# Six gate pairs as seven products each, with the operand sums made in DRAM

## The chip, the cores and the metric

The kernel runs on one core of one Trainium2 chip. The metric is the device time of one execution in microseconds (us). TensorE (PE) multiplies matrices into PSUM banks of 128x512 float32; VectorE (DVE), ScalarE (ACT) and GpSimd (POOL) work on tiles in SBUF; transfers are issued from the queues of SyncE (SP), ACT and POOL. In the profile, PEld is the loading of TensorE's weights.

## The reference

One hybrid decoder layer over 16 meta tokens and 1024 real tokens, D_MODEL = 1024, all in float32:

```
h = rmsnorm(concat(meta, x)) ;  proj = h @ w_in        # 1024 x 5128
u_pool, z_pool, q, k, v, z_attn, f_logit, g_pool, g_attn = split(proj)
y_pool = causal_multiscale_pool(u_pool) * silu(z_pool) # 4 groups, windows 2, 4, 8, 16
y_attn = forgetting_attention(q, k, v, log_sigmoid(f_logit + b)) * silu(z_attn)
merged = sigmoid(g_pool) * (y_pool @ w_up_pool) + sigmoid(g_attn) * (y_attn @ w_up_attn)
out = rmsnorm(residual + merged @ w_out)               # meta tokens dropped
```

The attention has 8 heads of 64, is causal, and adds a running sum of the log forget gates to each score. The two gates `g_pool` and `g_attn` are 1024 columns of `w_in` each; they are needed for the real tokens only.

## The kernel before, in words

Each float32 operand of a large product is split into a high part and a rest (`hi`, `lo`), and each product is made of three terms, hi·hi, hi·lo and lo·hi. The normalised tokens lie in SBUF transposed, as `hh4[j]` and `hl4[j]`: j is the half of the 1024 model dimensions, each tile holds 4 blocks of 128 dimensions by 1040 tokens. A column chunk of `w_in` (128 columns) is loaded by SP into `raw`, split by ACT (`whi`, L140) and POOL (`wlo`, L124, four pieces of 256), and multiplied in `g_proj` (L152) with 8 blocks x 3 terms = 24 matmuls for each 512 tokens: 48 for a chunk. `raw`, `whi` and `wlo` have two buffers each.

The work runs in these stages.

1. **Start** (to about 60 us): loading and normalising the tokens, the first pair of heads.
2. **Attention**: 16 units, one for each head and half of the tokens; a unit goes over 5 (first half) or 9 (second half) blocks of 128 keys. `qk` makes the scores of a block; ACT adds the gate sum (L581), on the diagonal blocks DVE does it with a causal mask (L579); DVE keeps the running maximum `m` (L588). `maxes` turns `m` into a maximum for each query with DVE transposes, a reduction and six small copies that swap partition halves and quarters (L597, L600). `soft` subtracts it (L612), ACT takes the exponential (L613) and the high part (L616), DVE the rest `pl` (L617), POOL adds up the row sums in `acc` (L625); `av` multiplies with V (L633). `finish` adds the two halves of `po` on DVE (L641) and stores them. The scores of unit i+1 are woven into `soft` of unit i (`merged`).
3. **Fill**: the order of TensorE's instructions is written by hand. Between the attention's steps the class `Fill` hands out single matmuls of other projections, as many nanoseconds as `PACE` times a cost figure of the step, less the step's own matmuls. The figures are 1.04·w+70 for a score step and 1.75·w+130 for a soft step of w columns. The free fill is, in this order: 4 chunks `u`, 4 `zp`, 8 `gp`, 8 `ga` (`f_u`, `f_raw`), whose results go by ACT into `st` (two buffers) and by SP to DRAM. `F.drain()` issues what is left when the attention has ended. The other engines' order is made by a planner from the program's order, dependencies and extra edges (`after`: order only; `behind`: a wait).
4. **Behind the attention**: the four `za` chunks (`f_za`), the pooling mixer (`pool_chain` adds shifted copies on DVE, `pool_split`, `pooled` multiplies), the row sums gathered (`fin`), `attn_norm`, `attn_gate`.
5. **Up projections**: 16 steps `up(j, a)` of 24 matmuls; a gate row is loaded from DRAM, its sigmoid is multiplied in; `G[j]` is the merged result. Sums of blocks of `G` and of `W` (`w_out`) are made on POOL and DVE (`t_first`, `t_second`, `s_first` ...).
6. **Output**: `merged @ w_out` is cut into 2x2 blocks and done by seven block products (n = 0 to 6, L995), not eight; `prep(n+1)` splits the next product's operands; then the residual, the norm and the stores.

Of the kernel before, what the change touches and what calls it, by code (L numbers as in the profile page):

```python
# [31 lines left out]
PACE = 2.05  # L32
# [20 lines left out]
def tile_hybrid_block(ctx, tc, x, meta, norm_g, w_in, b_forget, pool_w, pool_scale,  # L53
# [28 lines left out]
    mask = cst.tile([KB, KB], F32, name="mask")  # L82
    nc.vector.memset(mask, 0.0)
    nc.gpsimd.affine_select(out=mask, in_=mask, pattern=[[1, KB]], compare_op=ALU.is_ge, fill=NEG,
                            base=0, channel_multiplier=-1)
# [234 lines left out]
    def f_u(g):  # L320
# [3 lines left out]
        for c0, c1 in PIECES:  # L324
            ps = yield from g_proj(w, c0, c1)
            st = stg.tile([128, 512], F32, name="st")[:, :c1 - c0]
            nc.scalar.activation(st, ps, AF.Copy)
            nc.sync.dma_start(dt[:, c0:c1], st)
# [205 lines left out]
    for p in range(4):  # L534
        spill["y", p] = dr.tile([128, SEQ], F32, name=f"sp_y{p}")

    class Unit:
# [19 lines left out]
        def qk(self, b):  # L557
# [17 lines left out]
            f0 = max(d1, c0)  # L575
            if d1 > c0:
                j = t0 + c0 - b * KB
                mk = tail if own_keys else mask[:, j:j + d1 - c0]
                nc.vector.scalar_tensor_tensor(s[:kb, c0:d1], ps[:kb, c0:d1], nb_, mk, op0=ALU.add, op1=ALU.add)  # L579
            if f0 < 512:  # L580
                nc.scalar.activation(s[:kb, f0:], ps[:kb, f0:], AF.Identity, bias=nb_)  # L581
# [8 lines left out]
        def maxes(self, extra=0.0):  # L590
# [5 lines left out]
            for a, b in ((0, 64), (64, 0)):  # L596
                nc.vector.tensor_copy(x[a:a + 64], r[b:b + 64])  # L597
            nc.vector.tensor_tensor(r2, r, x, op=ALU.max)
            for a, b in ((0, 32), (32, 0), (64, 96), (96, 64)):
                nc.vector.tensor_copy(y[a:a + 32], r2[b:b + 32])  # L600
# [5 lines left out]
        def soft(self, b):  # L606
# [13 lines left out]
            if b == 1:  # L620
                if c0:
                    nc.gpsimd.tensor_copy(acc[:, :c0], S0[:, :c0])
                nc.gpsimd.tensor_tensor(acc[:, c0:], S0[:, c0:], s[:, c0:], op=ALU.add)
            elif b > 1:
                nc.gpsimd.tensor_tensor(acc[:kb, c0:], acc[:kb, c0:], s[:kb, c0:], op=ALU.add)  # L625
# [10 lines left out]
        def finish(self):  # L636
# [3 lines left out]
            nc.scalar.activation(t[hr], po[lr], AF.Copy)  # L640
            nc.vector.tensor_tensor(t[hr], po[hr], t[hr], op=ALU.add)  # L641
            nc.sync.dma_start(spill["y", self.p][hr, self.q0:self.q0 + 512], t[hr])
# [19 lines left out]
    raws = [(n, j) for n, c in (("zp", 4), ("gp", 8), ("ga", 8)) for j in range(c)]  # L662
# [3 lines left out]
    for key in raws:  # L666
        F.add_free(f_raw(key, cols[key[0]] + 128 * key[1]))

# [13 lines left out]
    for i, u in enumerate(units):  # L682
# [13 lines left out]
        u.finish()  # L696
        if nxt is not None and nxt.p != u.p:
# [45 lines left out]
    def f_za(p):  # L743
        w = w_chunk(COL_ZA + 128 * p)
        za[p] = btile("za")
        for c0, c1 in HALVES:
            ps = yield from g_proj(w, NM + c0, NM + c1)
            evacs.append(nc.scalar.activation(za[p][:, c0:c1], ps, AF.Silu))
# [42 lines left out]
    chains, yls = {}, []  # L791
    pool_chain(3)
    pool_chain(2)
    zp, za = [], {}
    for g in (3, 2, 1, 0):
        zp.append(reload(("zp", g)))
    zp.reverse()
    left = [f_za(p) for p in range(4)]

    def half_raw(g):  # L800
        for _ in range(3 * KO + 1):
            next(g)
# [15 lines left out]
    def gate_row(j, a):  # L818
        t = btile("rl")
        nc.sync.dma_start(t, spill[("gp", "ga")[a], j])  # L820
# [21 lines left out]
    for p in range(3):  # L842
        attn_in(p)
    half_raw(left[0])
    pool_split(3)
    run(left[0])
    split2 = pool_split(2)
    silu(zp[3])
    silu(zp[2])
    fin = sm.tile([128, 384], F32, name="fin", tag="fz", bufs=1)  # L850
    lall = fin[:, :256].rearrange("p (u a j) -> p u a j", u=4, a=4)
    rall = fin[:, 256:320]
    rect = fin[:, 320:].rearrange("p (b r) -> p b r", b=2)
    for p in range(4):
        nc.sync.dma_start(lall[32 * p:32 * p + 32],
# [254 lines left out]
```

## Time and profile before

| | |
|---|---|
| median of 3 runs | 744.66 us (744.38 to 744.8) |
| profiled execution: its time, its span | 743.96 us, 742.2 us |
| busy in the span: PE, PEld | 731.2 us (99%), 622.7 us (84%) |
| busy in the span: DVE, ACT, POOL | 533.2 us (72%), 377.0 us (51%), 332.8 us (45%) |
| DMA | 75.35 MB, mean 102 GB/s |
| granted TensorE clock | 0.997 |

How to read it: busy times are from the profiled execution alone, so sums are made against its 743.96 us; it is 0.70 us under the median. Matmuls are pipelined, so the mean duration of one matmul in a row (some 0.39 us) is longer than the distance from one to the next; a row with the total of many gives the distance.

### The profile page before, as it was taken

To read this page: it belongs to the slowest core of one execution; us is meant where nothing else is said; L and a number is where in the kernel's file an instruction comes from. 1 tells how busy PE (TensorE), PEld (TensorE's weight loads), DVE (VectorE), ACT (ScalarE), POOL (GpSimd) and SP (SyncE) were. 2 spreads that over 40 slices of the span, in tenths; PEclk is the share of its full clock that TensorE was granted. 3 is DMA by queue.
4 is the path that set the end of the run, shared out by engine and by line. 5 is a ranking of instruction groups with operands and counts; after the bars stand their busy time and mean duration, and the time that the engine had idled before them with its cause. 6 is when DMAs were issued, how large, how long until landed. Compare 5 with 4: busy or idle time off the path is not lost.

```text
span 742.2 us, 10619 instructions
## 1 busy us (share of the span) xinstructions
PE 731.2 (99%) x3686; PEld 622.7 (84%) x3686; DVE 533.2 (72%) x991; ACT 377.0 (51%) x736; POOL 332.8 (45%) x390
## 2 busy tenths in 40 slices
PE   8999999999999999999999999999999999999996
PEld 5997999988888898889988888888887888888885
DVE  5653577668779877688797687686288554997975
ACT  6662556446557545556563564452545322526445
POOL 4331235456426446345355383183348043606743
PEclk9999999999999999999999999999999999999998
DMA  9301132231312212222323223229375357360006
GB/s 301 88 15 43 29 86 86 62 98 23 95 48 60 80 50 90 78 53 55 94 66 86 80 80 92 72 81 309 95 201 212 142 200 240 116 224 1 1 0 227
DMA packets 76424, 75.35 MB, mean 102 GB/s; under 512 B 9665, under 2 KB 60865, under 8 KB 76370
## 3 DMA queue, kind: packets, MB, share of 16 engines
q1 hardware_dynamic: 74496, 69.95, 30.8%
q10 hardware_dynamic: 1874, 4.72, 1.7%
q8 instruction: 29, 0.48, 0.3%
q14 instruction: 25, 0.20, 0.1%
HBM read 55.58 MB, written 19.07 MB: 101 GB/s over the span
## 4 chain that ended last, share of the span: by engine, by line
PE 87%; DVE 5%; ACT 1%; issue 1%; POOLq 0%; POOL 0%; ACTq 0%
PE pj L152 65%; PE pj L995 8%; PE po L633 5%; PE ps L573 2%; PE ps L572 2%; PE pt L995 2%; PE pj L486 1%; DVE S L612 1%; DVE pl L617 1%; DVE ka L266 0%; PE pj L279 0%; DVE pt L603 0%; ACT S L581 0%; DVE mt L593 0%; ACT whi L140 0%
## 5 line engine op out<-in xcount | busy, mean ns | idle before, releaser
L124 POOL TENSOR_TENSOR wlo<-raw,whi 128x256 fp32r<-128x256 f32 x148 | 121.7, 852 | 192.5 <-ACT whi L140 96.1
L152 PE MATMUL pj<-hh,whi 128*128 128x512 f32 (+4 forms) x768 | 178.4, 360 | 0.6 <-ACT hh L201 0.3
L152 PE MATMUL pj<-hl,whi 128*128 128x512 f32 (+4 forms) x768 | 177.1, 359 | 0.0
L152 PE MATMUL pj<-hh,wlo 128*128 128x512 f32 (+4 forms) x768 | 174.4, 358 | 0.0
L152 PEld LDWEIGHTS pj<-hh,wlo 128*128 128x128 f32 x768 | 132.3, 188 | 18.1
L152 PEld LDWEIGHTS pj<-hh,whi 128*128 128x128 f32 x768 | 131.5, 188 | 18.7 <-ACT hh L201 0.5
L152 PEld LDWEIGHTS pj<-hl,whi 128*128 128x128 f32 x768 | 131.6, 188 | 17.7
L617 DVE TENSOR_TENSOR pl<-S,ph 128x512 fp32r<-128x512 f32 (+4 forms) x112 | 87.1, 792 | 19.3 <-ACT ph L616 18.8
L625 POOL TENSOR_TENSOR acc<-acc,S 128x272 f32<-128x272 f32 (+4 forms) x80 | 76.7, 958 | 11.2 <-ACT S L613 6.0
L581 ACT ACTIVATE S<-ps,negc 128x400 f32<-128x400 f32 (+2 forms) x96 | 49.3, 515 | 44.0 <-DVE S L579 35.7
L613 ACT ACTIVATE S<-S 128x512 f32<-128x512 f32 (+4 forms) x112 | 49.5, 478 | 33.7 <-DVE S L612 33.5
L616 ACT ACTIVATE ph<-S 128x512 fp32r<-128x512 f32 (+4 forms) x112 | 52.2, 480 | 15.8 <-PE po L633 14.4
L588 DVE TENSOR_TENSOR m<-m,S 128x272 f32<-128x272 f32 (+4 forms) x80 | 41.3, 517 | 23.8 <-ACT S L581 22.0
L140 ACT ACTIVATE whi<-raw 128x1024 fp32r<-128x1024 f32 x37 | 39.1, 1056 | 32.2 <-PE pj L152 27.8
L612 DVE TENSOR_TENSOR S<-S,pt 128x512 f32<-128x512 f32 (+4 forms) x112 | 51.9, 498 | 0.8
L836 DVE TENSOR_TENSOR rl<-pj,rl 128x512 f32<-128x512 f32 x32 | 22.0, 689 | 28.0 <-PE pj L152 28.0
L579 DVE SCALAR_TENSOR_TENSOR S<-ps,negc,mask 128x128 f32<-128x128 f32 (+2 forms) x72 | 23.7, 330 | 22.5 <-PE ps L573 22.3
L317 ACT ACTIVATE st<-pj 128x512 f32<-128x512 f32 x40 | 23.7, 593 | 28.1 <-PE pj L152 18.6
L633 PE MATMUL po<-pl,V 128*128 128x512 f32 (+4 forms) x112 | 37.6, 336 | 0.1
L573 PE MATMUL ps<-ql,ka 128*128 128x512 f32 (+4 forms) x112 | 37.5, 334 | 0.0
L572 PE MATMUL ps<-qa,ka 128*128 128x512 f32 (+4 forms) x112 | 36.0, 322 | 0.6 <-ACT S L581 0.5
L995 PE MATMUL pj<-opy 128*128 128x512 f32 (+1 forms) x168 | 36.3, 375 | 0.0
(187 smaller groups left out, 1134.2 us busy)
## 6 DMA issues: line engine op xcount, KB each, us to landing
raw<-in_w_in_dram SPq DMA_DIRECT2D x40, 512.0 KB, 3.9
sp_gp<-st SPq DMA_DIRECT2D x16, 256.0 KB, 2.0
sp_ga<-st SPq DMA_DIRECT2D x16, 256.0 KB, 2.0
rl<-sp_gp SPq DMA_DIRECT2D x8, 512.0 KB, 5.2
rl<-sp_ga SPq DMA_DIRECT2D x8, 512.0 KB, 4.5
W<-in_w_out_dram SPq DMA_DIRECT2D x8, 512.0 KB, 4.8
xr<-in_x_dram SPq DMA_DIRECT2D x8, 512.0 KB, 4.1
xt<-in_x_dram SPq DMA_DIRECT2D x7, 512.0 KB, 8.1
```

The lines of the kernel that those rows point to most:

```text
L124: ins = nc.gpsimd.tensor_tensor(out[:, c:c + 256], x[:, c:c + 256], y[:, c:c + 256], op=op)
L152: nc.tensor.matmul(ps, a, b, start=(i == 0), stop=(i == len(seq) - 1))
L572: nc.tensor.matmul(ps[:kb, c0:], ka[:, k0:k0 + kb], qa[:, q0 + c0:q0 + 512], start=True, stop=False)
L573: nc.tensor.matmul(ps[:kb, c0:], ka[:, k0:k0 + kb], ql[:, q0 + c0:q0 + 512], start=False, stop=True)
L581: nc.scalar.activation(s[:kb, f0:], ps[:kb, f0:], AF.Identity, bias=nb_)
L612: nc.vector.tensor_tensor(s[:kb, c0:], s[:kb, c0:], self.pm[:kb, c0:], op=ALU.subtract)
L613: exps.append(nc.scalar.activation(s[:kb, c0:], s[:kb, c0:], AF.Exp))
L616: nc.scalar.activation(ph[:kb, c0:], s[:kb, c0:], AF.Copy)
L617: dves.append(nc.vector.tensor_tensor(pl[:kb, c0:], s[:kb, c0:], r32(ph[:kb, c0:]), op=ALU.subtract))
L625: nc.gpsimd.tensor_tensor(acc[:kb, c0:], acc[:kb, c0:], s[:kb, c0:], op=ALU.add)
L633: nc.tensor.matmul(self.po[:, c0:], v, r[:kb, c0:], start=(b == 0 and i == 0), stop=(b == self.nb - 1 and i == 1))
L995: nc.tensor.matmul(ps, pick(A_, k, p)[:, i * 128:(i + 1) * 128], pick(B_, k, q)[:, c0:c1], start=start and n == 0, stop=n == 11, skip_grou ...
```

## The change

**Gates.** The 8 pairs of gate chunks (`gp` j, `ga` j) are cut: pairs 0 to 5 (`NP = 6`) are no longer two chunks of 48 matmuls. A pair is a 2x2 block product: rows gp and ga, the model dimension in two halves, the tokens in two halves. It is done by seven products of 12 matmuls (4 blocks x 3 terms, 512 tokens): A11·B11 (`q1`), A12·B21 (kept as `c11`), SD4·B22 (`x`), SD2·TT2, SD1·TT1, SD3·TT3, A22·TT4. Here SD1 = A21+A22, SD2 = SD1+A11, SD3 = A11+A21, SD4 = SD2+A12 are sums of the weights, and TT1 = B11-B12, TT2 = TT1+B22, TT3 = B12-B22, TT4 = TT3-B11+B21 sums of the tokens.

**Sums in DRAM.** `sums_of(i)` runs behind unit i. `put` is a copy from DRAM to DRAM on SP's queue, `add` a transfer on POOL's queue that adds onto its destination. The negated token halves (`negative`) are made by 12 DVE instructions of 128x512 through `st`. The same is done for the sums of `w_out` (TD1 to TD4), which were POOL's work in SBUF before; in the output stage the signs change to match. In all there are 17 `add`s for the sums, 4 that add the two halves of `po` (which `finish` now stores apart), and 6 in `join` behind the attention.

**Where the products go.** In the fill: 4 `u`, 4 `zp`, 4 `za`, 2 `gp`, 2 `ga` chunks, then SD4·B22 for two pairs at a time (`f_q3`, 3 times) and `q1`, `c11` (`f_q12`, 6 times); each of these nine has one weight split for 24 matmuls. Behind the attention: `t_prep` loads TT2, TT1, TT3, TT4 and overwrites the token halves with their splits; then 12 phases of 24 matmuls, with a weight split each, whose results are combined on DVE (`phase`) and stored; the pooling mixer and the norms are given out over the phases by the lists `todo` and `late`. `f_za` is gone from there.

**Off VectorE.** The mask is an `affine_select` on POOL after ACT's copy, except on a unit's own-keys block; the six swaps of `maxes` are ACT copies; the add in `finish` is gone. `PACE` goes from 2.05 to 1.7.

```diff
-PACE = 2.05
+PACE = 1.7
+NP = 6
...
+    def g_prod(w, n, kh, th, ps=None):
+        ...
+        t = slice(NM + 512 * th, NM + 512 * th + 512)
+        for i, (a, b) in enumerate((a, b) for a, b in ((0, hh4), (0, hl4), (1, hh4)) for _ in range(4)):
+            k = i % 4
+            nc.tensor.matmul(ps, w[a][:, 4 * n + k, :], b[kh][:, k, t], start=first and i == 0, stop=i == 11,
+                             skip_group_check=True)
+            yield mm_ns(512)
+        return ps
+    def f_q12(j):
+        w = w_chunk(COL_GP + 128 * j)
+        for n, key in enumerate(("q1", "c11")):
+            ps = yield from g_prod(w, n, n, 0)
+            keep(part[key][:, j], ps)
+    def f_q3(jj):
+        w = split_w([s_cols(4, 2 * jj), s_cols(4, 2 * jj + 1)])
+        for n in range(2):
+            ps = yield from g_prod(w, n, 1, 1)
+            keep(part["x"][:, 2 * jj + n], ps)
+        free_from.append(stores[-1])
...
+    def put(dst, src):
+        after(nc.sync.dma_start(dst, src), stores[-1])
+    def add(dst, src, **kw):
+        after(nc.gpsimd.dma_start(dst, src, accum_op=ALU.add, **kw), accs[-1])
+    def sums_of(i):
+        if i == 0:
+            put(SD[1], GB[2])
+            put(SD[3], GB[0])
+        elif i == 1:
+            add(SD[1], GB[3])
+        elif i == 2:
+            add(SD[3], GB[2])
+            put(SD[2], SD[1])
+            negative(TT[1], 0, 1)
+        ...
+        elif i == 8:
+            add(TT[2], side_h(hh4, 1, 1))
+            add(TT[4], TT[0], max_dma_last_dim=4096)
+        ...
+        if i % 4 == 3:
+            add(spill["y", i // 4], spill["yl", i // 4], max_dma_last_dim=4096)
...
-            if d1 > c0:
-                ...
-                nc.vector.scalar_tensor_tensor(s[:kb, c0:d1], ps[:kb, c0:d1], nb_, mk, op0=ALU.add, op1=ALU.add)
-            if f0 < 512:
-                nc.scalar.activation(s[:kb, f0:], ps[:kb, f0:], AF.Identity, bias=nb_)
+            if own_keys:
+                nc.vector.scalar_tensor_tensor(s[:, c0:], ps[:, c0:], nb_, tail, op0=ALU.add, op1=ALU.add)
+            else:
+                nc.scalar.activation(s[:, c0:], ps[:, c0:], AF.Identity, bias=nb_)
+                if d1 > c0:
+                    nc.gpsimd.affine_select(out=s[:, c0:d1], in_=s[:, c0:d1], pattern=[[1, d1 - c0]], ...)
...
-                nc.vector.tensor_copy(x[a:a + 64], r[b:b + 64])
+                nc.scalar.activation(x[a:a + 64], r[b:b + 64], AF.Copy)
...
+    def t_prep(n, kh, th):
+        t = slice(NM + 512 * th, NM + 512 * th + 512)
+        for h in range(2):
+            s = gp.tile([128, 2, 512], F32, name="ts", tag="g")
+            after(nc.sync.dma_start(s, TT[n][:, 2 * h:2 * h + 2]), free_from[-1])
+            hi = hh4[kh][:, 2 * h:2 * h + 2, t]
+            nc.scalar.activation(hi, s, AF.Copy)
+            nc.vector.tensor_tensor(hl4[kh][:, 2 * h:2 * h + 2, t], s, r32(hi), op=ALU.subtract)
+    PH = ((2, 0, 1), (1, 1, 1), (3, 0, 0), (None, 1, 0))
+    def phase(jj, i):
+        w = phase_weights(jj, i)
+        ...
+            if i == 0:
+                tt_(X[:, n], X[:, n], ps, op=ALU.subtract)
+            elif i == 1:
+                tt_(X[:, n], X[:, n], ps, op=ALU.add)
+            elif i == 2:
+                tt_(U[:, n], a, Q1[:, n], op=ALU.subtract)
+                tt_(U[:, n], U[:, n], R[jj][5 + n], op=ALU.subtract)
+            else:
+                tt_(Q1[:, n], a, Q1[:, n], op=ALU.subtract)
+        if i:
+            nc.sync.dma_start(part[("c12", "c22", "c21")[i - 1]][:, two], (X, U, Q1)[i - 1])
+    def join(jj):
+        two = slice(2 * jj, 2 * jj + 2)
+        for key in ("x", "c11"):
+            after(nc.gpsimd.dma_start(part[key][:, two], part["q1"][:, two], accum_op=ALU.add), los[-1])
...
+    todo = [[("split", 3), ("chain", 2)], [], [("silu", 3), ("gather",)], [("pooled", 3), ("split", 2), ("silu", 2)],
+            [("chain", 1), ("zp", 1)], [("pooled", 2), ("split", 1), ("ain", 0)], [("chain", 0), ("norm", 0), ("zp", 0)],
+            [("pooled", 1), ("split", 0), ("ain", 1), ("norm", 1), ("za", 0)]]
+    late = [[("gate", 0), ("ain", 2), ("norm", 2), ("za", 1)], [("pooled", 0), ("gate", 1), ("ain", 3), ("za", 2)],
+            [("norm", 3), ("gate", 2), ("za", 3)], [("gate", 3)]]
+    for n in range(count):
+        phase(n // 4, n % 4)
+        if n % 2 and 0 < (n + 1) // 2 < NP // 2:
+            join((n + 1) // 2)
+        for t in plan[n]:
+            fn[t[0]](*t[1:])
...
-        W[k] = hq.tile([128, D], F32, name="W", tag="w")
-        after(nc.sync.dma_start(W[k], wout[:, k, :]), muls[-1])
+    WSRC = [WB["11"], WB["21"], TD[2], TD[1], TD[3], WB["22"], TD[4]]
+    def w_load(n, h):
+        W[n, h] = hq.tile([128, 2, 512], F32, name="W", tag="w")
+        return nc.sync.dma_start(W[n, h], WSRC[n].rearrange("(k p) c -> p k c", p=128)[:, 2 * h:2 * h + 2])
```

More of the change, by code (lines that the diff above doesn't have):

```diff
@@ L696, in tile_hybrid_block @@
         u.finish()
+        sums_of(i)
         if nxt is not None and nxt.p != u.p:
@@ L791, in tile_hybrid_block @@
     chains, yls = {}, []
-    pool_chain(3)
[L793 to L802, printed above, removed]
+    def join(jj):
+        two = slice(2 * jj, 2 * jj + 2)
+        for key in ("x", "c11"):
+            after(nc.gpsimd.dma_start(part[key][:, two], part["q1"][:, two], accum_op=ALU.add), los[-1])
+    join(0)
+    t_prep(2, 0, 1)
+    t_prep(1, 1, 1)
+    t_prep(3, 0, 0)
+    t_prep(4, 1, 0)
+    pool_chain(3)
+    zp, za = {}, {}
+    for g in (3, 2):
+        zp[g] = reload(("zp", g))
     def pooled(g):
@@ L840, in up @@
             gt[j] = sg_
[L842 to L855, printed above, removed]
-                          sums[4 * p:4 * p + 4].rearrange("u (a r) j -> r u a j", r=32))
```

243 lines of the change are left out of this document (163 added, 80 removed).

## The prediction

> **What bounds the kernel now.** First the page's busy shares and its chain of waits, then a table of busy time by stage. Its columns: stretch, length, then busy time of PE, weight loads, DVE, ACT, POOL with instruction counts, granted clock, DMA share, GB/s.
>
> ```profile
> span 742.2 us, 10619 instructions
> ...
> PE 731.2 (99%) x3686; PEld 622.7 (84%) x3686; DVE 533.2 (72%) x991; ACT 377.0 (51%) x736; POOL 332.8 (45%) x390
> ...
> PE 87%; DVE 5%; ACT 1%; issue 1%; POOLq 0%; POOL 0%; ACTq 0%
> ```
> ```profile
> 60.00:503.00 443.00, 442.09 (x2274) 384.92 (x2272) 335.19 (x710) 238.21 (x491) 205.70 (x233) 1.00 0.25 70
> 503.00:519.00 16.00, 16.00 (x72) 13.01 (x71) 9.28 (x8) 3.92 (x6) 5.47 (x4) 1.00 0.89 304
> 519.00:569.00 50.00, 50.00 (x218) 40.60 (x217) 31.22 (x28) 22.04 (x29) 27.29 (x25) 1.00 0.50 149
> 569.00:659.00 90.00, 90.00 (x387) 72.03 (x386) 59.78 (x80) 35.43 (x47) 31.95 (x36) 1.00 0.57 197
> 659.00:742.00 83.00, 76.69 (x349) 63.52 (x347) 63.95 (x91) 40.74 (x88) 38.90 (x57) 0.98 0.19 70
> ```
>
> The stages are attention, drain, the work behind it, up projections, output. TensorE is busy for the whole of each but the last few microseconds, at full clock. That a busy TensorE is really what sets the time is read from its waits in the attention, and from a stretch of pure matmuls on the chain:
>
> ```profile
> PE ps L572 <- ACT S L581: 0.5, 1, 0.5
> PE pj L152 <- DVE V L285: 0.2, 1, 0.2
> ```
> ```profile
> 659.04 8.20 PE pj L995 x36
> ```
>
> It waits 0.7 us in 443. One 512-column matmul takes 8.20/36 = 0.2278 us, so the time is a count of matmuls, and taking work off DVE gains nothing by itself: nobody waits for DVE long enough to show. What the change can win is matmuls; what it can lose is this cover.
>
> **The matmuls.** Gates before: 16 chunks x 48 = 768. After: 4 chunks x 48 + 6 pairs x 7 x 12 = 696. That is 72 fewer, 72 x 0.2278 = **-16.4 us**. By place: the fill had 20 chunks (zp, gp, ga) = 960 and gets 12 chunks and 3 x 72 = 792, so -168; behind the attention the za chunks (192) go and 12 x 24 = 288 come, +96 (+21.9 us). Up and output keep their counts. The stages shift: the weave's cost figures sum to 128 us over all steps (37,888 columns of each kind), so 0.35 less PACE takes some 45 us of fill out of it. Counted step by step by the kernel's own rule, 1577 instead of 1782 fill matmuls are handed out before the last unit ends, and 106 instead of 69 are left to drain. So the attention ends 205 x 0.2278 = 46.7 us earlier (503 to 456), the drain takes 24.1 us instead of 15.7, the phases with the four pooling products (312 matmuls) 71.1 us instead of 49.2: up starts at 552, not 568. The stage behind the attention is 95 us instead of 65.
>
> **The attention, engine by engine.** Rows of the groups in 60 to 503 us (count | busy, mean ns | idle before), the select from the start:
>
> ```profile
> L581 ACT ACTIVATE S<-ps,negc 128x512 f32<-128x512 f32 x32 | 21.8, 685 | 8.1 <-PE ps L573 7.8
> ...
> L588 DVE TENSOR_TENSOR m<-m,S 128x512 f32<-128x512 f32 x24 | 18.8, 785 | 11.4 <-ACT S L581 11.0
> L579 DVE SCALAR_TENSOR_TENSOR S<-ps,negc,mask 128x128 f32<-128x128 f32 x48 | 16.7, 347 | 12.2 <-PE ps L573 11.9
> ...
> L600 DVE COPY my<-ms 32x16 f32<-32x16 f32 x64 | 11.2, 175 | 1.1
> ...
> L641 DVE TENSOR_TENSOR t<-po,t 64x512 f32<-64x512 f32 x15 | 10.3, 684 | 0.2
> L581 ACT ACTIVATE S<-ps,negc 128x400 f32<-128x400 f32 x16 | 9.4, 588 | 9.7 <-DVE S L579 9.7
> ...
> L597 DVE COPY mx<-mr 64x16 f32<-64x16 f32 x32 | 8.2, 255 | 0.8
> ...
> L613 ACT ACTIVATE S<-S 128x16 f32<-128x16 f32 x16 | 3.3, 208 | 3.2 <-DVE S L612 3.2
> ```
> ```profile
> L406 POOL TENSOR_TENSOR wlo<-raw,whi 128x1024 fp32r<-128x1024 f32 x3 | 7.1, 2381 | 2.0 <-ACT whi L401 2.0
> ...
> L84 POOL TENSOR_SCALAR_AFFINE_SELECT mask<-mask 128x128 f32<-128x128 f32 x1 | 0.3, 293 | 0.0
> ```
>
> DVE loses 72 masks (48 take 16.7 us; all, at this mean, at most 25), the swaps (19.4) and the 16 adds of `finish` (11), and gains 12 negations (0.785 each, as the nearest two-input row: 9.4). 335 becomes about 290 in 396 us, 73% as against 76%. ACT gains 72 times the 128 columns that DVE took (97 ns for 112 columns by the two rows: 8), 8 blocks more (2), 96 swaps of 0.208 (20): 238 becomes 268, 68% instead of 54%. POOL gains 72 selects x 0.293 = 21.
>
> POOL also issues 21 adding transfers here. No transfer on POOL's queue is in this trace. From below I take SP's issue of one (0.38 us, row further down), from above POOL's longest single operation, 2.4 us (L406): 8 to 50 us; I take 20, since a description of a transfer is nearer to an issue than to 131,072 subtractions. The nine fill chunks of 24 matmuls cost a split of POOL each where 48 used to share one; as four projections' worth less of fill remains, the splits go from 31 to about 28, -10 us. POOL: 206 to some 237, 60%.
>
> So means are no higher than 73%. But the weave is tighter: an odd unit (nine soft steps, five score steps) has cost figures of 8.85 us, so TensorE goes through it in 15.1 us, not 18.1. What it has in hand there is seen in the timeline, for units 13 and 5:
>
> ```profile
> 431.63 0.68 DVE L617 TENSOR_TENSOR pl<-S,ph 128x512 fp32r<-128x512 f32 x1
> ...
> 436.87 0.39 PE L633 MATMUL po<-ph,V 128*128 128x512 f32 x1
> ```
> ```profile
> 230.66 1.69 DVE L617 TENSOR_TENSOR pl<-S,ph 128x512 fp32r<-128x512 f32 x1
> 231.74 0.19 PEld L633 LDWEIGHTS po<-ph,V 128*128 128x128 f32 x1
> ...
> 232.40 0.19 PEld L633 LDWEIGHTS po<-pl,V 128*128 128x128 f32 x1 [0.48 <-DVE pl L617]
> ```
>
> Unit 13 has 4.6 us between `pl` and its use; unit 5, where the next pair's q, k and v also go through DVE, has none. The weave loses 3.1 us, its five masks give back 5 x 0.347 = 1.7: 1.4 us a unit. Unit 13 can pay this, units 5 and 9 can't: 2 x 1.4, taken as **+3 us**. Bounds: 0, and all eight odd units, 11.
>
> **Behind the attention.** Here POOL and DVE get more work in proportion than TensorE: 4.4 chunks of the drain and 12 phases need 16.4 splits in 95 us; before it was four. The question is whether the two can work side by side. Timeline rows, alone and together, and a DVE row alone:
>
> ```profile
> 519.41 2.83 POOL L124 TENSOR_TENSOR wlo<-raw,whi 128x256 fp32r<-128x256 f32 x4 [5.64 <-ACT whi L140]
> ...
> 558.19 6.76 POOL L124 TENSOR_TENSOR yl<-rl,yh 128x256 fp32r<-128x256 f32 x4
> 559.23 5.12 DVE L758 TENSOR_TENSOR y<-y,za 128x1024 f32<-128x1024 f32 x3
> ```
> ```profile
> L777 DVE TENSOR_TENSOR s<-s 128x1025 f32<-128x1025 f32 x1 | 1.2, 1226 | 0.0
> ```
>
> Four POOL pieces alone take 2.83 us, three such DVE operations 3.7: 6.5 together, and side by side they took 6.76. They take turns. The work that takes turns: POOL 16.4 + 4 (the `yl` pieces) times 2.83 = 58, six joins at 0.38, 2; DVE with both inputs in SBUF: 14 in the chains, 4 `pll`, 8 in `t_prep`, 8 norms and gates = 34 x 1.23 = 42. That is 102 us in 95. Some 4 us of norms and gates may slip into the up stage, which wants them only at its fifth step. The phases' 30 combining operations read PSUM and are left out. So 3 to 7, taken as **+5 us**; as low as 0 if turns overlap at their edges.
>
> The Trainium skill, page "SBUF — State Buffer", section "SBUF: two separate sides", has this as a rule: VectorE with two SBUF inputs and GpSimd share a port pair under an exclusive lock, and the loser waits for the whole instruction. By that rule, 102 - 95 = 7 us; these rows agree within 0.3 us in 6.5.
>
> Of transfers, this stage gets (MB): drain loads and stores 4, TT 4.2, u 2.1, zp and za 4.2, y and rc 4.2, phase weights 6.3, X and Q1 3.1, phase stores 4.7, joins 3.1, first up rows 1.6: 37.5. The rate in the busiest stretch before, and SP's rows:
>
> ```profile
> 506.00:522.00 16.00, 16.00 (x71) 12.98 (x70) 6.37 (x5) 5.20 (x6) 8.06 (x8) 1.00 0.94 320
> ```
> ```profile
> raw<-in_w_in_dram SPq DMA_DIRECT2D x40, 512.0 KB, 3.9
> ```
> ```profile
> 499.35 0.38 SPq L136 DMA_DIRECT2D raw<-in_w_in_dram  x1
> ```
>
> 320/0.94 = 340 GB/s when full: 110 us for a stage of 95. About 4 MB can lie outside (two of the four TT, one u before; the last stores behind), which leaves 98 us, hidden beside the turns. A raw chunk takes 3.9 us to land and has two buffers, so it needs no free queue, only one not more than a phase (5.5 us) behind. Bounds 0 and +15. The phases' stores wait on DVE in SP's queue, and the next phases' weights stand behind them: this is where a late DVE reaches TensorE.
>
> **Nothing** is taken for the rest: the W sums leave POOL, which sat at 32 of 90 us in the up stage; loads of W come later in stages with DMA shares of 0.57 and 0.19. They are covered by 387 and 349 matmuls; uncovered, a W load is some 4 us.
>
> **Sum.** 742.2 - 16.4 + 3 + 5 = 733.8 of span; with 1.8 us around it (743.96 less 742.2) 735.6; the median lies 0.7 above the profiled run: **736 us**.
>
> **Rivals.** *Everything is covered*: the matmuls alone, 744.66 - 16.4 = 728. For it: 0.7 us of waits now, means under 75%. Against: unit 5. Chance 0.22. *The transfers bound the stage behind the attention*: 110 us and not 95, +15, +3 in the attention: 746; with each join counted as read and written (3.1 MB more, 9 us) 755. For it: shares of 0.89 and 0.94 already with half the bytes. Against: TensorE did not wait then, and loads can be early. It decides from a stretch of 13 us. Chance 0.17. *POOL's queue holds the attention*, the slower side: the select now stands between ACT's copy and DVE's maximum, and on POOL it can stand behind a split (up to 3.3 us) and an adding transfer (2.4, or longer if its `put` hasn't landed, since the queue is in order). 5.7 us against the 3.2 (4.6 - 1.4) that an odd unit has left: 2.5 x 8 = 20, with the +8 above: 756. Against: splits were in that queue before, and TensorE had 4.6 in hand. It decides from 4.3 us of delay a unit. Chance 0.11. That the change doesn't do what it says is no rival for the matmuls: they are counted out in the code.
>
> **Numbers.** The forecast, with a stretch of 3 to 13 us (731 to 742), has 0.50. About 0.2%, 1.5 us, is what this measurement can tell from no change: same is 743.2 to 746.1. The transfers' case gives 0.02 faster, 0.07 same, 0.08 slower; POOL's 0.01 same, 0.10 slower. Faster 0.74, same 0.08, slower 0.18. The range goes from 727 (all covered, less a little) to 750, which leaves out the far ends of the two slow cases, some 0.15.
>
> **What would show it.** Right: TensorE instructions down by some 72; attention's last `po` near 460; up from about 557 to 562; waits of TensorE on DVE's `pl` in units 5 and 9, on `wlo` or on DVE's combinations in the phases. Wrong: a DMA share near 1 through the phases with loads landing in over 8 us; selects late on POOL and TensorE waiting in `po` in most odd units; or no wait at all.

## The result: 821.26 us, a tenth slower, and the profile after

The kernel after takes 821.26 us (816.69 to 822.97), 1.102 times the kernel before, with a 95% interval of 1.097 to 1.107. The forecast was 736, its range ended at 750. From here on "the stage behind" means the time from the attention's last `po` to the first `up`, that is the drain and the phases.

The page of the kernel after: its first rows, the DMA queues (q0 holds the adding transfers that POOL issues, q1 those of SP's queue), and the chain:

```profile
span 821.3 us, 11051 instructions
PE 741.2 (90%) x3614; PEld 625.1 (76%) x3614; DVE 526.8 (64%) x856; ACT 419.0 (51%) x855; POOL 370.1 (45%) x492
DMA packets 110091, 140.91 MB, mean 172 GB/s; under 512 B 11841, under 2 KB 72257, under 8 KB 109906
q1 hardware_dynamic: 97424, 108.23, 41.9%
q0 software_dynamic: 10160, 25.17, 17.8%
PE 53%; DMA 13%; DVE 8%; POOL 7%; issue 6%; ACT 6%; SPq 1%; POOLq 0%; ACTq 0%; DVEq 0%
```

TensorE has its 72 matmuls fewer (3614, not 3686), yet is busy for 741.2 us. Without any loss its busy time would be 731.2 - 16.4 = 714.8 and its idle time the 11.0 of before (742.2 - 731.2). So the span of 821.3 lies 95.5 above 725.8, in two parts: 69.1 more idle (80.1 against 11.0), and 26.4 of matmuls that took longer. The granted clock answers for the second: it stands at half for 67 us of the span, against 4 before. And transfers are now on the chain with 13%, where there were none.

The table of busy time by stage (us, busy time and count of PE, weight loads, DVE, ACT and POOL, then granted clock, DMA share, GB/s): attention, drain, the hole before the first phase, phases with the pooling.

```profile
60.00:492.00 432.00, 407.65 (x2069) 354.57 (x2068) 303.30 (x537) 257.47 (x587) 230.56 (x314) 0.97 0.63 151
...
492.00:528.00 36.00, 26.68 (x107) 21.01 (x106) 4.91 (x4) 12.69 (x18) 13.68 (x20) 0.91 0.96 294
528.00:539.00 11.00, 0.97 (x5) 0.45 (x3) 2.94 (x3) 2.81 (x4) 0.00 (x0) 0.71 1.03 293
539.00:648.00 109.00, 82.43 (x312) 63.62 (x313) 67.73 (x69) 33.68 (x38) 66.99 (x68) 0.87 0.81 243
```

Each stage against the count of its matmuls: the attention ends at 492 and not at 456; the drain lasts 36 us and not 24.1; then TensorE has nothing for 11 us; the phases last 109 us and not 71.1. That is 36 + 12 + 11 + 38 = 97 us (95.5 by the spans), all of it between the first unit and the first `up`. From the first `up` (648) to the end it is 173 us, as before.

What TensorE waited for, in the same kernel (us in total, times, longest):

```profile
PE pj L915 <- ACT whi L137: 21.2, 4, 10.5
PE pj L336 <- ACT st L343: 9.3, 2, 6.2
PE pj L915 <- DVE U L905: 8.1, 2, 7.4
PE po L743 <- DVE pl L727: 7.7, 8, 1.7
PE ps L681 <- ACT S L687: 6.9, 4, 5.3
```

The two largest are waits of the phases for split weights and of the drain for an evacuation. ACT is not slow there: a split of raw weights takes it 1.05 us, as before. The pieces of transfer in the chain of waits say who is late (start, length):

```profile
158.18 8.58 DMA tt<-st
...
204.06 8.03 DMA tt<-st
...
218.20 6.01 DMA tt<-st
```
```profile
505.75 4.62 DMA part_c<-st
511.10 10.18 DMA part_c<-st
522.01 4.97 DMA part_c<-st
528.09 10.20 DMA raw<-sd
552.23 9.84 DMA u<-sp_u
569.34 10.81 DMA raw<-sd
```

And the list of issues (KB each, median us from issue to landing):

```profile
raw<-in_w_in_dram SPq DMA_DIRECT2D x34, 512.0 KB, 5.2
...
raw<-sd SPq DMA_DIRECT2D x24, 256.0 KB, 4.9
...
tt<-st SPq DMA_DIRECT2D x12, 256.0 KB, 6.0
u<-sp_u SPq DMA_DIRECT2D x4, 520.0 KB, 9.8
```

A chunk of raw weights took 3.9 us before and takes 5.2 now; `u` took 4.9 and takes 9.8. The prediction had named its refutation: a share near 1 through the phases with loads landing in over 8 us. That came in the drain and the hole (0.96, 1.03, raw weights in 10.2 us). In the phases the share was 0.81; there `u` and `Q` (the reloaded `q1`) landed that late (medians 8.1 and 8.9 us), the weights in 5.3, at worst 10.8.

### The profile page after: what moved, and what is told of

Same layout as the page of the kernel before. It is cut to its first block, busy times and chain, and to the rows that moved or that the text cites. A ratio compares the mean times of both kernels' runs of the same rounds, so it can differ in the third digit from the quotient of the medians.

```text
span 821.3 us, 11051 instructions
## 1 busy us (share of the span) xinstructions
PE 741.2 (90%) x3614; PEld 625.1 (76%) x3614; DVE 526.8 (64%) x856; ACT 419.0 (51%) x855; POOL 370.1 (45%) x492
## 3 DMA queue, kind: packets, MB, share of 16 engines
q1 hardware_dynamic: 97424, 108.23, 41.9%
q0 software_dynamic: 10160, 25.17, 17.8%
## 4 chain that ended last, share of the span: by engine, by line
PE 53%; DMA 13%; DVE 8%; POOL 7%; issue 6%; ACT 6%; SPq 1%; POOLq 0%; ACTq 0%; DVEq 0%
PE pj L149 31%; PE pj L1160 7%; POOL wlo L121 4%; PE pj L336 3%; DMA raw<-sd 3%; PE pj L915 3%; PE po L743 3%; DMA tt<-st 3%; DMA part_c<-st 2%; DVE pl L727 2%; PE pt L1160 2%; PE ps L682 1%; DMA tt<-tt 1%; PE ps L681 1%; DMA u<-sp_u 1%
## 5 line engine op out<-in xcount | busy, mean ns | idle before, releaser
L121 POOL TENSOR_TENSOR wlo<-raw,whi 128x256 fp32r<-128x256 f32 x184 | 152.1, 913 | 148.8 <-ACT whi L137 134.8
L149 PE MATMUL pj<-hh,whi 128*128 128x512 f32 (+4 forms) x576 | 130.5, 357 | 4.0 <-DVE S L722 2.4
L149 PE MATMUL pj<-hh,wlo 128*128 128x512 f32 (+4 forms) x576 | 130.5, 353 | 0.0
L149 PE MATMUL pj<-hl,whi 128*128 128x512 f32 (+4 forms) x576 | 128.6, 351 | 0.0
L149 PEld LDWEIGHTS pj<-hh,wlo 128*128 128x128 f32 x576 | 98.8, 193 | 10.0
L149 PEld LDWEIGHTS pj<-hl,whi 128*128 128x128 f32 x576 | 97.5, 191 | 9.9
L687 ACT ACTIVATE S<-ps,negc 128x512 f32<-128x512 f32 (+4 forms) x104 | 57.5, 560 | 33.8 <-PE ps L682 33.1
L915 PE MATMUL pj<-hh,whi 128*128 128x512 f32 x96 | 30.3, 443 | 34.9 <-ACT whi L137 21.2
L915 PEld LDWEIGHTS pj<-hh,whi 128*128 128x128 f32 x96 | 19.6, 212 | 41.9 <-ACT whi L137 28.9
L689 POOL TENSOR_SCALAR_AFFINE_SELECT S<-S 128x128 f32<-128x128 f32 (+2 forms) x72 | 25.7, 391 | 51.1 <-ACT S L687 50.6
L743 PE MATMUL po<-ph,V 128*128 128x512 f32 (+4 forms) x112 | 37.5, 335 | 2.6 <-ACT ph L726 2.6
## 6 DMA issues: line engine op xcount, KB each, us to landing
sd<-in_w_in_dram POOLq DMA_DIRECT2D x4, 1536.0 KB, 13.8
```

The source lines that it names most:

```text
L121: ins = nc.gpsimd.tensor_tensor(out[:, c:c + 256], x[:, c:c + 256], y[:, c:c + 256], op=op)
L149: nc.tensor.matmul(ps, a, b, start=(i == 0), stop=(i == len(seq) - 1))
L687: nc.scalar.activation(s[:, c0:], ps[:, c0:], AF.Identity, bias=nb_)
L743: nc.tensor.matmul(self.po[:, c0:], v, r[:kb, c0:], start=(b == 0 and i == 0), stop=(b == self.nb - 1 and i == 1))
L915: nc.tensor.matmul(ps, w[a][:, 4 * n + i % 4, :], b[kh][:, i % 4, t], start=first and i == 0, stop=i == 11, skip_group_check=True)
```

## The experiments

The table gives the main quantities of all runs. "Transfers" is the busy time of the 16 DMA engines in the stage behind, from the packets' records; for the kernel after it can be worked out from the rows above, share times length: 0.96 x 36 + 1.03 x 11 + 0.81 x 109 = 134 us. The packets' times overlap a little, as the share of 1.03 shows. "Drain" includes the hole before the first phase. The times are medians, the stages come from one profiled execution each. The kernel after ran in 816.7 to 823.0 us and its profile is the slowest of these, so differences of a few us between two rows show nothing by themselves.

| run | time, us | ratio to before | last `po` | drain | phases | transfers |
|---|---|---|---|---|---|---|
| after | 821.3 | 1.102 | 492 | 47 | 109 | 134 |
| b_offv | 747.0 | 1.003 | - | - | - | - |
| a_nosum | 791.2 | 1.062 | 462 | 47 | 107 | 132 |
| a_negput | 799.4 | 1.073 | 470 | 47 | 107 | 132 |
| a_np4 (8 phases) | 818.1 | 1.099 | 484 | 70 | 89 | 131 |
| a_wonce | 789.2 | 1.061 | 493 | 48 | 77 | 111 |
| a_noload | 791.9 | 1.064 | 489 | 47 | 78 | 110 |
| a_notprep | 818.4 | 1.100 | 490 | 34 | 119 | 119 |
| a_lean | 794.9 | 1.068 | 493 | 35 | 92 | 94 |
| a_st4 | 810.3 | 1.090 | 480 | 47 | 108 | 132 |
| a_ahead | 818.1 | 1.099 | 494 | 47 | 105 | 137 |
| a_st4ahead | 808.9 | 1.087 | 482 | 48 | 104 | 139 |
| a_best | 798.5 | 1.072 | 482 | 45 | 98 | 129 |
| a_st4notprep | 804.5 | 1.081 | 482 | 31 | 114 | 119 |
| a_bare | 762.5 | 1.024 | 481 | 29 | 81 | 77 |
| a_barenosum | 742.9 | 0.998 | 463 | 31 | 74 | 73 |

**The masks and swaps alone (b_offv).** The kernel before with the masks and the swaps of "Off VectorE" alone. `PACE` stays 2.05, and `finish` keeps its add:

```diff
-                nc.vector.scalar_tensor_tensor(s[:kb, c0:d1], ps[:kb, c0:d1], nb_, mk, op0=ALU.add, op1=ALU.add)
...
+                nc.scalar.activation(s[:, c0:], ps[:, c0:], AF.Identity, bias=nb_)
+                if d1 > c0:
+                    nc.gpsimd.affine_select(out=s[:, c0:d1], in_=s[:, c0:d1], pattern=[[1, d1 - c0]],
...
-                nc.vector.tensor_copy(x[a:a + 64], r[b:b + 64])
+                nc.scalar.activation(x[a:a + 64], r[b:b + 64], AF.Copy)
```

> The kernel before with only the masks (a select on GpSimd behind ScalarE's copy) and the six swaps (ScalarE) taken off VectorE; PACE 2.05, gates and all transfers as before. Theory T, late transfers (the stores from the two `st` buffers and the weight loads land late because the sums in DRAM and the loads behind the attention crowd the DMA queues; ScalarE and VectorE then wait in order, TensorE idles and runs at half clock after it): no change, 743 to 747 us. Theory P, GpSimd's queue (the select behind splits and sums makes the maximum late): slower by 5 us or more here already, TensorE waiting in po or ps.

746.96 us, 1.0031 [1.0019, 1.0044]: 2.3 us slower, and no wait of TensorE above 1.3 us. A select behind the splits in POOL's queue holds nobody for long. The rival in which POOL's queue holds the attention falls as far as masks and splits go; the adding transfers in that queue are in the next runs.

**The sums in the attention (a_nosum, a_negput).** First without any of them, then with all but the negations:

```diff
 def sums_of(i):
-        if i == 0:                         # a_nosum: every copy, add and negation goes
-            put(SD[1], GB[2])
...
-            negative(TT[1], 0, 1)          # a_negput: a plain copy for each negated half
+            put(TT[1], w_in2[:, :4, 0:512])
...
```

> The changed kernel without any sum in DRAM: no put, no add, no negation; the products read blocks of w_in and w_out in place of the sums (so the numbers computed are others), with the same count of matmuls, splits and of loads behind the attention. Only the four adds of the attention's halves and the joins stay. Theory T: the attention's last po moves from 492 us to 460 to 470, the stage behind it stays near 150 us long (its own loads and stores are all there): about 795 us. Theory P: the selects and the tighter weave remain, so the last po stays above 480: about 810 us.

> The changed kernel with its 12 negations by VectorE left out: the three negated halves are filled by one copy each from DRAM to DRAM (of other data, so the numbers are others), all further sums as they were. Theory T in the form that the shared `st` buffers are the door: the idle stretches of TensorE between 158 and 222 us go, and the attention ends some 15 us earlier: about 805 us. If the traffic as such slows everything, or GpSimd's queue: within 5 us of 821.

Without sums the attention ends at 462, where the prediction had it at 456 + 3. Masks on POOL, swaps on ACT, the tighter weave: those terms of the sum were right within 3 us, in size; where the waits fall is taken up below. The row of its attention, and what TensorE waited for there:

```profile
60.00:462.00 402.00, 397.65 (x2072) 347.61 (x2071) 283.87 (x525) 257.29 (x587) 213.15 (x298) 1.00 0.27 75
```
```profile
PE pj L149 <- DVE S L676: 2.4, 1, 2.4
PE ps L635 <- ACT S L641: 1.1, 3, 0.5
PE po L697 <- DVE pl L681: 0.8, 2, 0.5
```

TensorE idles 4 us there, against 24 with the sums (432.00 - 407.65 above), and the mean clock is 1.00. So the sums cost 30 us, and DVE's share was not the reason (283.87 of 402 against 303.30 of 432). With plain copies of the same size in place of the twelve negations the attention ends at 470: 22 of the 30 us belong to the negations. The other 8 are all that the sums' copies and adding transfers cost it, POOL's queue included. The negations go through the two `st` buffers, which also carry the evacuations of the fill. The rows of the tile `st` in the kernel after, 140 to 240 us (who waited for it, us and times):

```profile
DMA to landing us min/median/max: 1.9/5.2/8.6
```
```profile
  DVE st L593: 11.6, 4
  ACT st L314: 8.7, 1
```

A store from `st` that lands after 5 to 8.6 us keeps a buffer for that long. The next negation on DVE, or the next evacuation on ACT, stands in its engine's queue in front of the soft steps' work, and TensorE waits for those. Both runs came out as theory T has it, a_negput with more than the 15 us expected.

**Four `st` buffers (a_st4).**

```diff
-    gp  = ctx.enter_context(tc.tile_pool(name="gp", bufs=13))
-    stg = ctx.enter_context(tc.tile_pool(name="stg", bufs=2))
+    gp  = ctx.enter_context(tc.tile_pool(name="gp", bufs=12))
+    stg = ctx.enter_context(tc.tile_pool(name="stg", bufs=4))
```

> The kernel after, with four `st` buffers in place of two (negations, y's parts and the products that are kept go through them) and 12 in place of 13 `g` buffers to make the room. Theory B (the two buffers are what the stores' longer landing is felt through): last po at 472 to 480 in place of 492, drain 24 to 30 us in place of 36, the stretch behind as before; 795 to 808. Rival (the DMA engines' bytes set the pace, the buffers only show it): last po 486 to 492 and drain 33 to 37, or what they win comes back in the phases; 814 to 822.

810.28 us, 1.0895 [1.0834, 1.0957]. In the attention, theory B holds: last `po` at 480, 12 us earlier. In the drain it falls: 36 us as before, with a hole of 10 behind. The total lies between the ranges of the two theories. ACT's timeline in that drain shows other releasers, `t_prep`'s loads and a weight load:

```profile
487.14 1.06 ACT L869 ACTIVATE hh<-ts 128x1024 fp32r<-128x1024 f32 x1 [10.44 <-DMA ts<-tt]
...
506.68 1.06 ACT L869 ACTIVATE hh<-ts 128x1024 fp32r<-128x1024 f32 x1 [8.20 <-DMA ts<-tt]
...
525.84 1.06 ACT L137 ACTIVATE whi<-raw 128x1024 fp32r<-128x1024 f32 x1 [9.67 <-DMA raw<-sd]
```

ACT waits in order for a transfer that is not in, and the evacuation that TensorE needs stands behind it. The two stalls cover for each other.

**Without t_prep (a_notprep), and without it and with four buffers (a_st4notprep).** Both leave out `t_prep`, so the phases multiply other numbers.

```diff
-    t_prep(2, 0, 1)
-    t_prep(1, 1, 1)
-    t_prep(3, 0, 0)
-    t_prep(4, 1, 0)
```

> The changed kernel without t_prep: the token sums are not loaded and split behind the attention (the phases multiply the tokens as they are), so 4.2 MB of loads, 8 operations of ScalarE and 8 of VectorE go, nearly all of them from the drain. Theory C: the drain's stores land in 3 us, not 5 to 10, the drain shrinks from 36 to about 26 us and the first phase follows it at once: total 800 to 805. Theory L: the drain shrinks by that, the phases don't: 805 to 812.

> The kernel after with four `st` buffers (12 `g` buffers) and without t_prep, so the phases multiply other numbers than they should. Theory C (each of the two alone left the other to hold the drain): drain 24 to 28 us, last po to up 138 to 148, total 795 to 804. Rival (something third holds the drain): drain 31 us or more, total 804 to 812.

a_notprep: 818.38 us. Drain and hole go from 47 to 34, and the phases from 109 to 119: nearly all is given back, and both theories fall. a_st4notprep: 804.53 us, drain 31.0. Its drain is 3 us shorter than without `t_prep` alone and sits on the rival's edge of 31: the cover was there, but it is not all. A third thing holds the drain; a_barenosum below shows it.

**Weights loaded once (a_wonce), and split each time (a_noload).** In a_wonce the first phase's weights serve all twelve; in a_noload they are loaded once and split anew by ACT and POOL for every phase.

```diff
 def phase_weights(jj, i):
-    n = PH[i][0]
...
-    return split_w([s_cols(n, 2 * jj), s_cols(n, 2 * jj + 1)])
+    if "w" not in R:                                  # a_wonce
+        R["w"] = split_w([s_cols(2, 0), s_cols(2, 1)])
+    return R["w"]
```

> The changed kernel with one weight load and one split for all 12 phases (the later phases reuse the first one's, so the gates computed are others): 11 loads of 0.5 MB, 11 splits of ScalarE and 11 of GpSimd fewer behind the attention, matmuls as before. Now 155 us lie between the last po and the up projections, where 95 us are matmuls. Theory L (a loop of load, ScalarE's split and GpSimd's split over two raw buffers, some 17 us for two phases, sets the pace of the phases): 105 to 115 us, total 770 to 782. Theory C (the bytes crowd all transfers; the loop is only one victim): 130 to 140 us, total 795 to 806.

> The same, but each phase splits anew from one raw tile that is loaded once: the 11 loads are gone, all splits stay. If in the loop the load is the long part (5 to 10 us): close to the kernel with one split, within 8 us. If the turns of GpSimd and VectorE are: it stays 15 us or more above it, near 800 us.

a_wonce: 789.24 us, stage behind 125, between the ranges of both theories. a_noload: 791.90 us, 2.7 above it, as it should be if the load is the long part. The rows of the phases, first a_wonce, then a_noload:

```profile
540.00:617.00 77.00, 75.40 (x312) 60.74 (x313) 56.92 (x67) 22.73 (x28) 23.99 (x24) 0.96 0.84 259
```
```profile
537.00:615.00 78.00, 75.71 (x313) 59.27 (x314) 64.60 (x68) 33.16 (x38) 74.02 (x68) 0.98 0.83 260
```

POOL goes from 24 to 74 us of 78, busy all through, beside DVE with 65, and the phases grow by one and a half us. So the splits and the turns of POOL and DVE, for which the prediction charged 5 us, cost some 1.5 us here. POOL has next to nothing to spare in that stage, so what the turns would cost beside 71 us of bare matmuls is not shown. The eleven loads, 5.8 MB, cost 31 us of phase: the 24 us by which the transfers' busy time falls (134 to 110 in the table), and 7 more.

**Fewer pairs (a_np4), and no joins (a_lean).** a_lean leaves out `t_prep`, the joins, and the loads of X and Q1 (set to zero).

```diff
-NP = 6
+NP = 4                                                # a_np4
```
```diff
-    join(0)                                           # a_lean, beside t_prep; the later joins too
...
-            nc.sync.dma_start(R[jj][0], part["x"][:, two])
+            nc.gpsimd.memset(R[jj][0], 0.0)                 # the same for Q1
```

> The changed kernel with four pairs by seven products, not six (NP = 4): 24 matmuls more than with six (+5.5 us), four phases fewer behind the attention. Theory T: the stage from the attention's end to the up projections shrinks from 155 us in proportion to its loads, by 30 to 40 us, with the attention hardly changed: 785 to 795 us. If the stage behind were bound by VectorE and GpSimd taking turns, as the prediction had it: it shrinks by the turns of four phases, some 12 to 15 us: about 810 us.

> The changed kernel without t_prep, without the six joins and without the loads of X and Q1 (GpSimd zeroes them): 10.4 MB of some 38 fewer behind the attention, three of them in adding transfers; weights and stores stay. Theory C: the stage shrinks from 155 us to 110 to 120: 780 to 787 us. Theory L: weights are the pace still, 135 us or more: 800 us or more.

a_np4, 818.07 us: a third less of the change's products, hardly anything won, and both theories missed. They left out where the matmuls go: the drain has 225 of them, not 105, and the stage 441, not 417. With these and 131 us of transfers it lasts 158, as with six. a_lean, 794.86: the stage falls from 156 to 127, which neither theory had. Its transfers, 94 us, take no longer than its 95 us of matmuls, and it still lost 32 us. So "the longer of transfers and matmuls" is the wrong model.

**Order in SP's queue (a_ahead, a_st4ahead).** In the kernel after, a phase's load can stand behind the store of the phase before. SP's timeline there:

```profile
617.76 0.45 SPq L922 DMA_DIRECT2D rc<-recs  x1
625.32 0.32 SPq L910 DMA_DIRECT2D part_c<-X  x1
...
627.12 1.20 SPq L133 DMA_DIRECT2D raw<-sd  x2
```

By POOL's timeline the raw buffer for phase 10 was free at 612, but the load is issued at 627, behind a store; the store waits for DVE, DVE for the phase before, and phase 10 then starts 7 us after its load is issued (634). a_ahead asks for the weights one phase earlier in the program:

```diff
 def phase(jj, i):
-    w = phase_weights(jj, i)
+    w = pws.pop(0)
+    if 4 * jj + i + 1 < 2 * NP:
+        pws.append(phase_weights((4 * jj + i + 1) // 4, (i + 1) % 4))
```

> The kernel after, with the weights of a phase asked for one phase earlier in the program, ahead of the phase's stores and of the other loads in SP's queue; same transfers, same two raw buffers. Theory O (the order of SP's queue: a load stands behind stores that wait for the phase before): phases 80 to 92 us in place of 108.7; 793 to 806. Rival (bytes: the same transfers take the same time in any order): phases 100 to 112; 813 to 824.

> Both edits of the two runs beside it. Theories B and O together: 768 to 790, last po 472 to 480, drain 24 to 30, phases 80 to 92. Rivals (bytes): above 805.

818.08 and 808.91 us. The phases go from 109 to 105 and 104 us, the totals by less than these kernels scatter: theory O falls, the order of these loads is worth 4 us at most. Waits that vanish at one place turn up at another: in a_ahead those for split weights fall from 21.2 to 13.8 us, those for DVE's `U` rise from 8.1 to 15.2.

**Packets of 1 KB (a_best).**

```diff
-    nc.sync.dma_start(raw[:, k0:k0 + s.shape[1], :], s)      # two of [128, 4, 128]
+    nc.sync.dma_start(raw, src)                              # one of [128, 4, 256]
```

> The run a_st4ahead (808.9 us), and the weights of a pair of chunks loaded as one transfer with runs of 1 KB in place of two with 512 B. 512 B packets took 30.6 ns and 2 KB packets 95.0 ns on queue q1 in the kernel after; 1 KB packets should take 45 to 52 ns in place of 61 for the same bytes, 0.3 to 0.5 us of all engines for each of the twelve loads. Theory S (packets matter): 798 to 806. Rival (no): 806 to 812.

798.53 us, 1.0720 [1.0702, 1.0739], 10 us below a_st4ahead, as theory S has it. 1 KB packets took 54.1 ns in the mean and 46 in the median, against 30.6 and 27 for 512 B: over 7,680 packets and 16 engines that is 3.4 us of engine time in the whole kernel. The gain is larger; half of SP's issues for these loads are gone too, and which of the two brought the rest was not separated. This is the fastest of the variants that do the whole change, and it stays 54 us behind the kernel before.

**Without the transfers (a_bare, a_barenosum).** All matmuls and combinations stay; a_bare is a_lean with four `st` buffers and one weight load and split; a_barenosum also drops the sums, negations included.

> The kernel after with four `st` buffers (12 `g` buffers), without t_prep, without the joins, X and Q1 set to zero in place of their loads, and one weight load and split for all twelve phases: all matmuls and combinations are kept, the numbers are not. About 70 us of transfers are left in the stage, under the 95 us of its matmuls. Theory T (the transfers hold the stage): last po to up 95 to 104 us, last po 478 to 482, total 748 to 760. Rival Q (the queues' order or the engines' turns hold a part of their own): 112 us or more, total 768 or more.

> The run a_bare, and no sums in the attention either (no copies, adding transfers or negations there; the products read blocks of the weights as they are). Theory T: last po 459 to 463, last po to up 95 to 104, total 727 to 738, what the prediction gave with everything covered. Rival: 748 or more.

a_bare: 762.53 us, stage behind 110. That is between the theory's 95 to 104 and the rival's 112. a_barenosum: 742.94 us, 0.9976 [0.9956, 0.9995], stage 104.5; the time lies between the theory's 738 and the rival's 748. A row of its page and its two stages:

```profile
PE 720.3 (97%) x3614; PEld 612.3 (83%) x3614; DVE 490.2 (66%) x836; ACT 400.9 (54%) x836; POOL 312.2 (42%) x431
```
```profile
463.00:495.00 32.00, 28.49 (x115) 22.06 (x114) 7.12 (x8) 11.03 (x17) 22.79 (x27) 0.95 0.78 228
495.00:568.00 73.00, 71.70 (x310) 57.90 (x309) 49.29 (x59) 19.55 (x23) 16.82 (x18) 1.00 0.66 220
```

With these transfers gone the phases are TensorE's again: 71.70 busy of 73, full clock. By the spans, 81 of the 95 us of loss are gone (821.3 to 740.2). Not all of it need be the transfers': the negations, `t_prep`'s work on ACT and DVE and eleven splits went too, and two `st` buffers came. a_noload bounds the splits at some 1.5 us; the rest was not taken apart. What is left, 14.4 us over the matmul count (740.2 against 725.8), is 8.9 of idle time and 5.5 of slower matmuls. The largest single wait is in the drain. ACT's timeline:

```profile
477.15 0.36 ACTq L783 DMA_DIRECT2D rl<-sp_zp  x1
477.61 0.60 ACT L343 ACTIVATE st<-pj 128x512 f32<-128x512 f32 x1 [6.30 <-DMA sp_yl<-t]
```

A reload on ACT's queue takes memory that the attention's last `t` still holds; it waits 6.3 us for the store of `t`, and an evacuation stands behind it, for which TensorE waits 3.2 us. This is the third thing in the drain; in a_st4notprep the same wait took 6.36 us of ACT and 3.3 of TensorE.

## Why the prediction was wrong, by its steps

**The bound** was read rightly for the kernel before: nothing but matmuls. That this cover would carry the change was the error.

**The matmuls**: 72 fewer, as counted. But a kernel with these matmuls, and with most of the change's transfers left out, takes 742.9 us and not 728: the case "everything is covered" was not reached even there: the tighter weave, the drain and the transfers that remain give back 14 of the 16.4 us.

**The attention, +3.** Selects, swaps and the weave of the prediction held in size (462 without sums, 459 forecast). That the +3 fits is luck in part: the waits for `pl` that it was made of, 2.8 us in units 5 and 9, came to 0.8 in all in a_nosum. The step that failed is the price of the sums: negations were charged as 9.4 us of DVE, adding transfers as 20 us of POOL issuing them. As busy times these were near: 8.7 us for the negations, 24 for the 21 issues. Neither their stores' hold on the two `st` buffers nor their load on the DMA engines had a term. Measured: 30 us, 22 of them from the negations. Two more buffers give back 12. How the other 10 of the 22 divide between waits on queues and the crowd of transfers was not tried.

**The turns of POOL and DVE, +5.** The turns are real in the rows, but phases with twelve splits (78 us) are only some 1.5 us longer than phases with one (77). So the choice of the turns over the transfers as the thing that binds was wrong. Whether the term of 5 us is wrong by itself stays open: even with one split, the phases lasted 77 us and not 71.

**The transfers, 0 to +15.** This was the rival "the transfers bound the stage behind", at 746 to 755 with a chance of 0.17; it named the right cause, and its size was off by a factor of four: 61 us over the 95 of matmuls, not 15. Bytes were near (37.5 MB counted, 40.3 measured). The rate was not: 340 GB/s was worked out from a stretch of loads and stores; here 40.3 MB in 134 us of busy engines are 302. By its model, the longer of transfers and matmuls, 134 us would still be only 39 over; the other 22 come on top. The step that failed is the cover given to the weights: "it needs no free queue, only one not more than a phase (5.5 us) behind", with a landing of 3.9 us. The phases are a chain: load, split, matmul, combine, store. A 256 KB load takes 5 to 11 us among the others, and a store can stand ahead of it in SP's queue, so it can be more than a phase late, as phase 10's was. Then TensorE idles, drops to half clock and runs the next matmuls at half speed.

**How a us of transfers turns into time.** The runs in the table with one and the same matmul count go from 73 us of transfers in the stage and a length of 104.5 (a_barenosum) to 134 and 156 (after): 61 us of transfers cost 51, 0.84 each, and not only from 95 on as the model of the prediction had it. This is a mean between two ends, not a price: eleven weight loads gave back 31 for 24, `t_prep` 4 for 15, and a_lean with 94 us of transfers takes 2 us longer than a_noload with 110. So it matters which transfer goes. Why the two ends lie so near to a sum was not settled: fewer transfers land sooner and also mean fewer queue waits, and the runs change both at once.

**The drain, 24.1.** It was counted rightly as 106 matmuls, but charged with no wait. It has three kinds of wait, which stand behind one another on ACT: the `st` buffers, `t_prep`'s loads, and the reload that waits for the attention's memory. Taking one away shows the next.

**The chances.** 0.18 for slower was held by two cases of +1 to +11 us, each with one place. None let several stalls share one cause, the load on the DMA engines, in the attention, the drain and the phases at once.

## What to carry to other kernels

A stage that is all matmuls hides transfers only as long as they land well before their use: before doubling the traffic of such a kernel (75 to 141 MB here), price each load's landing time under the new load and each in-order queue that it stands in, not only bytes over peak rate. When matmuls are traded for sums in memory, count the passes: 16.4 us of matmuls were bought with 66 MB of traffic and 268 us of busy DMA engines (all queues: 62.3% of 821.3 us, against 32.9% of 742.2), and little of it had free cover where it was wanted. When a buffer is shared between a hot path and a new use, the new use's store latency becomes the hot path's.

## What the runs showed of the hardware that was not expected

**Adding transfers took about twice the engine time per byte.** In the rows of the two queues of the kernel after, 25.17 MB on q0 took 17.8% of the engines and 108.23 MB on q1 41.9%: 0.71 against 0.39% for a MB, 1.8 times. Packet by packet, 2 KB took 195 ns on q0 and 95 on q1. All transfers on q0 add, so whether the adding or the queue costs this was not separated.

**A short idle time can halve the clock for longer than it lasted.** In the windows view, first a_st4, then a_bare, two stretches each at the same place of the attention:

```profile
370.18:373.60 3.42, 1.39 (x10) 1.02 (x9) 3.42 (x8) 2.05 (x6) 3.01 (x3) 1.00 0.02 7
373.60:377.01 3.41, 3.05 (x7) 2.48 (x8) 1.73 (x5) 2.99 (x9) 3.17 (x6) 0.50 0.02 7
```
```profile
371.45:374.87 3.42, 1.91 (x14) 1.54 (x13) 3.42 (x6) 2.04 (x6) 3.02 (x3) 1.00 0.53 198
374.87:378.28 3.41, 2.53 (x11) 2.12 (x12) 1.74 (x6) 3.41 (x10) 3.25 (x5) 1.00 0.03 7
```

Some 2 us of idle time cost 3.4 us at half clock in one (7 matmuls) and nothing in the other. The difference is where it fell. In each run, all changes of the clock lie on one grid of 3.41 us. In a_st4 the idle time lay inside one step of the grid, of which TensorE was busy for 1.39 of 3.42 us; in a_bare it was split over two, busy for 1.91 and 2.53. Over the kernel after and all variants, half clock followed each of the 98 full-clock steps from 60 us on that were under 43% busy, and none that was over 65% busy; between the two it went either way. In the kernel after, longer holes cost 6.8 to 10.2 us at half clock. The Trainium skill, page "TensorE: Matmul & The Clock Gate", section "What's actually happening", gives half rate as the state after at least one idle window of about 3.4 us. The lengths measured, 3.4, 6.8 and 10.2 us, agree; that the step need not be idle throughout is what these runs show beside it. The prediction had no term for this, and 26 us of slower matmuls came.
